# Unequal gaps between the eight split weight buffers of a two-block transformer kernel

## The chip, the cores and the metric

The kernel runs on one core of a Trainium2 chip. The metric is the device time of one launch in microseconds (us); the time before is the median of three runs. Traces are of one profiled execution of the same program.

## The reference

Two transformer blocks over 256 tokens of 2048 features, all in float32. Cut to the products that matter here:

```python
h = modulate(rmsnorm(x, g_norm_mix[l]), shift_m, scale_m)
proj = h @ w_in[l]                        # q, k, v of two kinds of attention
...
x = x + gate_m[:, None, :] * (jnp.concatenate([o_diff, o_mla], axis=-1) @ w_out[l])
h = modulate(rmsnorm(x, g_norm_ffn[l]), shift_f, scale_f)
f = jnp.square(jax.nn.relu(h @ w_ff1[l])) @ w_ff2[l]
...
xn = _rms(x, norm_attn[l])                # second block
... = jnp.split(xn @ w_in[l], points, axis=-1)
merged = jax.nn.sigmoid(gate_a) * (o_a @ w_up_fox[l]) + jax.nn.sigmoid(gate_b) * (o_b @ w_up_nsa[l])
x = x + merged @ w_out[l]
hn = _rms(x, norm_ffn[l])
x = x + (jax.nn.silu(hn @ w_ffn_gate[l]) * (hn @ w_ffn_up[l])) @ w_ffn_down[l]
```

All weight matrices together are some 550 MB, and each is used once for all 256 tokens.

## The kernel before

Weights stream through in tiles of 128 partitions by up to 1024 float32 numbers, 512 KB each, in the order of one list (`plan`). `load` issues the transfer of a tile from SyncE into a raw buffer. `split_next` makes two parts of it in the type float32r: ScalarE copies the raw tile into `wh` (line 117, the high part), and VectorE subtracts (line 118: `wl = raw - wh`, the low part). `get` hands a split tile to `linear`, and splits the tiles behind it ahead of their use.

`linear` holds two accumulators in PSUM, one for each 128 tokens (`tt`). For each split tile, for both `tt` and for both halves `kk` of the tile (each holds 128 rows of the weight, 512 columns wide or fewer), `mm3` issues three matmuls (lines 132, 133, 134): high activation by high weight, high activation by low weight, low activation by high weight. So one tile makes 12 matmuls in a row, in four rounds of three. The activation, 128 columns, is the stationary operand (`lhsT`); the weight is the moving one (`rhs`), of 512 columns or fewer. Every matmul has a weight load (LDWEIGHTS) of its own, which TensorE does while the matmul ahead of it streams. In the trace a matmul reads `acc<-wh,Ah`: output, moving operand, stationary operand.

The activations are held split too, as pairs: `Ah`, `Al` (the normalized input of a projection), `midh`, `midl` and `mid2h`, `mid2l` (the hidden layers of the two feed-forward parts), `O2h`, `O2l` (attention output of the second block), `Mh`, `Ml` (the merged heads). One product has the roles reversed: in `q_nope` the activation `cqh`, `cql` moves, 256 columns, and the weight is stationary. Attention itself uses plain float32 operands.

Buffers lie in SBUF one behind another in the order in which their pools are opened. The split weight buffers are four `wh` and four `wl` of 4096 bytes a partition, in the pool `whl`; behind it come the pools of `x`, of `Ah` and `Al`, of small tiles, and those of each stage. A pool with several buffers of one tag deals them out in turn. The start of each in bytes, as the built program has it:

| tiles | first start | modulo 512 | modulo 64 |
|---|---|---|---|
| `wh` (4), `wl` (4), each 4096 behind the one ahead | 46368, 62752 | 288 | 32 |
| `Ah`, `Al` | 95520, 111904 | 288 | 32 |
| `cqh`, `midh`, `midl`, `mid2h`, `mid2l`, `O2h`, `O2l`, `Mh`, `Ml` | 191424, 180160, 196544, 141248, 157632, 133056, 149440, 165824, 182208 | 448 | 0 |

Slices within a tile begin at multiples of 64 bytes behind its start; those of the 512-column weight tiles and of the 128-column stationary operands at multiples of 512.

Of the kernel before, what the change touches and what calls it, by code (L numbers as in the profile page):

```python
# [9 lines left out]
F32 = mybir.dt.float32  # L10
# [6 lines left out]
P = 128  # L17
# [15 lines left out]
class HL:  # L33
    """A float32 operand held as the exact sum of two float32r parts."""
# [8 lines left out]
class Kernel:  # L43
    def __init__(self, ctx, tc, a, out, offs):
        self.tc, self.nc, self.a, self.out, self.offs = tc, tc.nc, a, out, offs
        self.ctx = ctx
        pool = lambda name, bufs, **k: ctx.enter_context(tc.tile_pool(name=name, bufs=bufs, **k))
        self.const = pool("const", 1)
        self.wraw = pool("wraw", RAW_BUFS)
        self.whl = pool("whl", SPLIT_BUFS)  # L50
        self.xp = pool("xp", 1)
        self.ap_ = pool("ap", 1)
        self.sm = pool("sm", 4)
        self.ps_acc = pool("ps_acc", 4, space=bass.MemoryType.PSUM)
        self.ps_tr = pool("ps_tr", 2, space=bass.MemoryType.PSUM)
        self.ps_at = pool("ps_at", 2, space=bass.MemoryType.PSUM)
        ctx.enter_context(tc.manual_schedule())
        self.fillers = []
        self.done = set()
        self.now = 0  # L60
        self.budget = 2
        self.ahead = 2

    # ---------------------------------------------------------------- helpers
# [16 lines left out]
    def rsqrt(self, ms, n, tag, pool=False):  # L81
        """ms ** -0.5: a first guess from the exponent, then three Newton steps."""
        v = self.nc.vector
        e = self.nc.gpsimd if pool else v
        ti = self.tiny("rs_i", n, I32)
        v.tensor_scalar(ti, ms.bitcast(I32), 1, None, op0=OP.logical_shift_right)
        y = self.tiny(tag, n)
        v.tensor_scalar(y.bitcast(I32), ti, -1.0, 1597463007.0, op0=OP.mult, op1=OP.add)
        h = self.tiny("rs_h", n)
        v.tensor_scalar(h, ms, -0.5, None, op0=OP.mult)  # L90
        t = self.tiny("rs_t", n)
        cols = [slice(i, i + 1) for i in range(n)]
        for _ in range(3):
            if n <= 2:
                for c in cols:
                    e.tensor_scalar(t[:, c], y[:, c], y[:, c], h[:, c], op0=OP.mult, op1=OP.mult)  # L96
                for c in cols:
                    e.tensor_scalar(y[:, c], t[:, c], 1.5, y[:, c], op0=OP.add, op1=OP.mult)  # L98
            else:
                e.tensor_mul(t, y, y)  # L100
                e.tensor_mul(t, t, h)
                if pool:
                    e.tensor_scalar(t, t, 1.5, None, op0=OP.add)
                    e.tensor_mul(y, y, t)
                else:
                    v.scalar_tensor_tensor(y, t, 1.5, y, op0=OP.add, op1=OP.mult)
        return y
# [6 lines left out]
    def split(self, dst, src, scale=None):  # L114
        """dst (HL) = src * scale, rounded to its two parts."""
        if scale is None:
            self.nc.scalar.activation(dst.hi, src, AF.Copy)  # L117
            self.nc.vector.tensor_sub(dst.lo, src, dst.hi.bitcast(F32))  # L118
        else:
            self.nc.scalar.activation(dst.hi, src, AF.Copy, scale=scale)  # L120
            self.nc.vector.scalar_tensor_tensor(dst.lo, src, scale, dst.hi.bitcast(F32),
                                                op0=OP.mult, op1=OP.subtract)
# [6 lines left out]
    def mm3(self, out, x, w, start, stop):  # L129
        """out += x.T @ w from the parts of x and w."""  # L130
# [9 lines left out]
    # ---------------------------------------------------------- weight stream  # L140
    def start_stream(self, plan):
        self.plan = plan
        self.dma_ptr = 0
        self.split_ptr = 0
        self.use_ptr = 0
        self.raw = {}
        self.ready = {}
        self.load()
# [14 lines left out]
    def split_next(self):  # L163
# [6 lines left out]
        else:  # L170
            hi = self.whl.tile([P, 1024], F32R, tag="wh", name="wh")
            lo = self.whl.tile([P, 1024], F32R, tag="wl", name="wl")
# [15 lines left out]
    def get(self):  # L188
        """The next weight tile; the ones behind it are split ahead of their use."""
# [6 lines left out]
    # ------------------------------------------------------ the conditioning  # L196
    def ada_part(self, e, src):
        """One tile of w_ada: feature by partition on VectorE, or k by partition on TensorE."""
# [36 lines left out]
    def row_of(self, sec, pool):  # L235
        """A gate, held feature by partition, as the same row in every partition."""
# [14 lines left out]
    # -------------------------------------------------------------- schedule  # L251
# [42 lines left out]
    # ------------------------------------------------------------- linear job  # L294
    def linear(self, groups, w, evac, acc=None, first=True, last=True, needs={}):
        """acc[tt] += sum over the groups' k tiles; groups: lists of HL [128, 256]."""
# [20 lines left out]
    # ------------------------------------------------------------------ setup  # L317
# [67 lines left out]
    def rope(self, x, cos, sin, slots, tmp):  # L385
        """x [128, slots, 2h] in place; cos, sin [128, 2h]; tmp [128, 2, slots, 2h]."""
# [10 lines left out]
    # ---------------------------------------------------- norm and modulation  # L397
# [4 lines left out]
    # ================================================================ block 1  # L402
    def x_hat(self, kg, r, xh):
        """512 features of the normalized x."""
# [4 lines left out]
    def x_hat_T(self, b, xh):  # L409
        """Two feature tiles of xh, transposed in one bank."""  # L410
# [6 lines left out]
    def modulate(self, A, kt, n, src, which, h):  # L417
        """A[:, kt .. kt + n - 1] = the two parts of src * scale + shift."""
# [25 lines left out]
    def block1_attention_proj(self):  # L444
# [12 lines left out]
        with ExitStack() as e2:  # L457
# [112 lines left out]
            # q_nope of all heads, transposed  # L570
# [12 lines left out]
            # q_rope  # L583
# [45 lines left out]
    def p_transpose_evac(self, blocks, dst, n):  # L629
        """blocks: (column offset, in_) transposed into one bank; dst [*, n] copied from it."""  # L630
# [42 lines left out]
    def diff_head(self, h, pj, O, wp, kab):  # L673
# [54 lines left out]
        for tt in range(2):  # L728
            junk = wp.tile([P, P], F32, tag="jk", name="jk", bufs=2)
# [12 lines left out]
    def block1(self):  # L742
# [26 lines left out]
        # output projection, in the order in which the heads end  # L769
# [46 lines left out]
    def ffn1(self, r):  # L816
# [46 lines left out]
        def ff1_start():  # L863
            """The first three column blocks, a quarter of their rows at a time."""
# [63 lines left out]
    def r12_gen(self, ss):  # L928
        """The two norms of x, the second from the first: r1 and r1 * r2."""
# [23 lines left out]
    def xT_gen(self, A, j, gain, key):  # L953
        """A[:, 4j .. 4j+3] from the 512 columns of x, times the gain."""
# [12 lines left out]
    # ================================================================ block 2  # L967
# [21 lines left out]
    def rms_heads(self, pj, n, heads, key, width):  # L989
        """pj [128, 2, >= n * width] in place: each of n heads of width normalized."""  # L990
# [14 lines left out]
    def key_gen(self, pj, kcat, br, gain, key):  # L1005
        """ks or kw: normalize, transpose into kcat[:, g, kb, (kt, br, 128)]."""
# [15 lines left out]
    def flat_gen(self, src, F, nt, kind, key):  # L1022
        """F (HL [128, nt, 48]) = the blocks of the compression, feature-major."""
# [475 lines left out]
    # -------------------------------------------------------------- the order  # L1499
    def make_plan(self):  # L1500
# [19 lines left out]
        def even(main, side):  # L1520
            """side spread evenly over main."""
# [71 lines left out]
def insert2(s, step):  # L1593
    """Every step-th column of s [128, n]."""
# [9 lines left out]
def layout(inp):  # L1604
    """The inputs as the program reads them: values moved, none changed."""
# [15 lines left out]
    A = {}  # L1621
# [111 lines left out]
```

## Time and profile before

| | before |
|---|---|
| time, median of 3 runs (lowest, highest) | 2742.49 us (2740.55, 2745.44) |
| span of the profiled execution, first to last instruction | 2742.6 us |
| TensorE matmul busy | 2675.7 us, 98% |
| TensorE weight load busy | 2219.3 us, 81% |
| VectorE, ScalarE, GpSimd busy | 1699.0, 1244.4, 82.9 us |
| mean granted TensorE clock | 0.991 of 2.4 GHz |

The span of the profiled execution equals the median to 0.1 us, so a sum made against the one holds for the other. A matmul's busy time in the trace reaches from its start to its modelled end, and matmuls overlap: how long one takes in a row of many is read from the distance of two starts, not from its busy time.

### The profile page before, as it was taken

Reading aid. Unit: us, or ns where it says so; the run is one execution under the profiler, and the core shown is the slowest. Engines: PE = TensorE matmul, PEld = TensorE weight load, DVE = VectorE, ACT = ScalarE, POOL = GpSimd, SP = SyncE. Lnnn points to the kernel's source line nnn. Section 1 sums busy time; section 2 is a strip of 40 time slices with the busy share of each in tenths; the row PEclk is TensorE's granted clock in tenths of the full one; section 3 lists DMA queues with packets and bytes.
Section 4 is the critical chain, followed back from the end, with each engine's and each line's share of the span. In section 5 each row is a group of like instructions: output and inputs, shape, how many; then the busy total and the mean of one; then the engine's idle time right before and its main releaser. Section 6 shows DMA issues by size and latency. Waiting matters only on the chain.

```text
span 2742.6 us, 34412 instructions
## 1 busy us (share of the span) xinstructions
PE 2675.7 (98%) x12646; PEld 2219.3 (81%) x12646; DVE 1699.0 (62%) x2761; ACT 1244.4 (45%) x1791; POOL 82.9 (3%) x151
## 2 busy tenths in 40 slices
PE   7999999899999999999999999999999999999999
PEld 3588977688888888878898998888888888888887
DVE  5587877866666555667766665555554545454555
ACT  3255654344444444454655554444444343434443
POOL 0002320000000000002000000000000000000000
PEclk9999999999999999999999999999999999999999
DMA  9977777667777655545733555656556665666564
GB/s 351 331 268 272 262 256 276 243 225 234 232 236 231 215 191 185 183 163 161 251 124 99 162 180 181 189 190 189 180 188 188 187 192 188 190 189 192 185 191 146
DMA packets 163608, 568.85 MB, mean 207 GB/s; under 512 B 18288, under 2 KB 18544, under 8 KB 162800
## 3 DMA queue, kind: packets, MB, share of 16 engines
q1 hardware_dynamic: 160992, 558.70, 61.6%
q10 hardware_dynamic: 2448, 7.97, 0.7%
q8 instruction: 99, 1.62, 0.2%
q14 instruction: 69, 0.57, 0.1%
HBM read 564.50 MB, written 2.10 MB: 207 GB/s over the span
## 4 chain that ended last, share of the span: by engine, by line
PE 83%; DVE 6%; issue 4%; ACT 3%; POOL 2%; DMA 2%; SPq 0%; ACTq 0%; DVEq 0%; POOLq 0%
PE acc L133 25%; PE acc L132 25%; PE acc L134 25%; PE tr L138 2%; DVE wl L118 2%; POOL rs_t L96 2%; PE tr L206 2%; ACT wh L117 1%; DVE ajunk L222 1%; DMA raw<-ada_scale_m 1%; PE at L1160 1%; POOL r_d L98 0%; DMA raw<-ff 0%; DMA x<-x 0%; PE at L132 0%
## 5 line engine op out<-in xcount | busy, mean ns | idle before, releaser
L118 DVE TENSOR_TENSOR wl<-raw,wh 128x1024 fp32r<-128x1024 f32 (+3 forms) x926 | 1071.5, 1164 | 831.7 <-ACT wh L117 826.1
L117 ACT ACTIVATE wh<-raw 128x1024 fp32r<-128x1024 f32 (+3 forms) x926 | 930.7, 1011 | 982.8 <-PE acc L134 917.7
L132 PE MATMUL acc<-wh,Ah 128*128 128x512 f32 (+2 forms) x2400 | 912.8, 380 | 6.7 <-ACT Ah L117 5.1
L133 PE MATMUL acc<-wl,Ah 128*128 128x512 f32 (+2 forms) x2400 | 896.0, 373 | 8.3 <-DVE wl L118 8.2
L134 PE MATMUL acc<-wh,Al 128*128 128x512 f32 (+2 forms) x2400 | 895.2, 373 | 0.5 <-DVE Al L118 0.5
L132 PEld LDWEIGHTS acc<-wh,Ah 128*128 128x128 f32 x2400 | 453.7, 189 | 84.7 <-issue 10.2
L133 PEld LDWEIGHTS acc<-wl,Ah 128*128 128x128 f32 x2400 | 453.8, 189 | 76.3 <-DVE wl L118 12.1
L134 PEld LDWEIGHTS acc<-wh,Al 128*128 128x128 f32 x2400 | 453.2, 189 | 66.4 <-DVE Al L118 2.0
L133 PE MATMUL acc<-wl,midh 128*128 128x512 f32 x512 | 204.2, 399 | 0.8 <-DVE wl L118 0.8
L132 PE MATMUL acc<-wh,midh 128*128 128x512 f32 x512 | 202.8, 396 | 0.3 <-ACT midh L117 0.2
L222 DVE SCALAR_TENSOR_TENSOR ajunk<-raw,silu_row 128x1024 bf16<-128x1024 f32 x160 | 195.1, 1219 | 12.2 <-ACT silu_row L249 10.6
L134 PE MATMUL acc<-wh,midl 128*128 128x512 f32 x512 | 201.2, 393 | 0.0
L133 PE MATMUL acc<-wl,mid2h 128*128 128x512 f32 x352 | 140.5, 399 | 0.0
L132 PE MATMUL acc<-wh,mid2h 128*128 128x512 f32 x352 | 139.2, 395 | 0.0
L134 PE MATMUL acc<-wh,mid2l 128*128 128x512 f32 x352 | 138.0, 392 | 0.0
L132 PEld LDWEIGHTS acc<-wh,midh 128*128 128x128 f32 x512 | 96.1, 188 | 25.0 <-ACT midh L117 0.5
L133 PEld LDWEIGHTS acc<-wl,midh 128*128 128x128 f32 x512 | 96.2, 188 | 23.4 <-DVE wl L118 1.6
L134 PEld LDWEIGHTS acc<-wh,midl 128*128 128x128 f32 x512 | 96.1, 188 | 23.3 <-DVE midl L118 0.4
L132 PEld LDWEIGHTS acc<-wh,mid2h 128*128 128x128 f32 x352 | 66.1, 188 | 17.0
L134 PEld LDWEIGHTS acc<-wh,mid2l 128*128 128x128 f32 x352 | 66.1, 188 | 15.8
L133 PEld LDWEIGHTS acc<-wl,mid2h 128*128 128x128 f32 x352 | 66.1, 188 | 15.0
L133 PE MATMUL acc<-wl,O2h 128*128 128x512 f32 (+1 forms) x208 | 73.3, 352 | 0.3 <-DVE wl L118 0.3
(430 smaller groups left out, 2159.8 us busy)
## 6 DMA issues: line engine op xcount, KB each, us to landing
raw<-ff SPq DMA_DIRECT2D x256, 512.0 KB, 4.3
raw<-f2g SPq DMA_DIRECT2D x88, 512.0 KB, 3.6
raw<-f2u SPq DMA_DIRECT2D x88, 512.0 KB, 3.6
raw<-f2d SPq DMA_DIRECT2D x88, 512.0 KB, 3.8
raw<-wo SPq DMA_DIRECT2D x64, 512.0 KB, 4.3
raw<-wi_d SPq DMA_DIRECT2D x64, 384.0 KB, 4.4
raw<-w_fox SPq DMA_DIRECT2D x64, 384.0 KB, 3.3
raw<-ada_scale_m SPq DMA_DIRECT2D x32, 512.0 KB, 6.8
```

The costliest lines, as they stand in the source:

```text
L96: e.tensor_scalar(t[:, c], y[:, c], y[:, c], h[:, c], op0=OP.mult, op1=OP.mult)
L117: self.nc.scalar.activation(dst.hi, src, AF.Copy)
L118: self.nc.vector.tensor_sub(dst.lo, src, dst.hi.bitcast(F32))
L132: mm(out, lhsT=x.hi, rhs=w.hi, start=start, stop=False)
L133: mm(out, lhsT=x.hi, rhs=w.lo, start=False, stop=False)
L134: mm(out, lhsT=x.lo, rhs=w.hi, start=False, stop=stop)
L138: self.nc.tensor.transpose(out, in_, self.ident[0:n, 0:n])
L206: self.nc.tensor.matmul(self.ada_row[0:1, :], lhsT=self.silu_c[:, kt:kt + 1], rhs=src[:, kk * 512:(kk + 1) * 512], start=kt == 0, stop=kt ...
L222: v.scalar_tensor_tensor(junk, src, 1.0, self.silu_row[:, (k % 2) * 1024:(k % 2 + 1) * 1024], op0=OP.mult, op1=OP.mult, accum_out=self.ada ...
L1160: mm(ps1, lhsT=qT[:, kb, P:T], rhs=kcat[:, g, kb].rearrange("p t b k -> p (t b k)"), start=kb == 0, stop=kb == 1)
```

## The change

The pool `whl` no longer deals out four buffers of each tag. It holds eight tiles of their own names (`wha`, `wla`, `whb`, ... `wld`), taken in turn by a counter, and ahead of six of them lies an empty tile of 32 to 192 bytes. The gaps make 544 bytes together; all pools behind `whl` begin 544 bytes later. To make room for them, a scratch tile of 512 bytes (`jk`, line 729, the squares of an attention output on ScalarE, of which only the sum is used) has one buffer in place of two. Comments and docstrings went as well, which moves line numbers: lines 132 to 134 are 133 to 135 in the changed kernel, 117 and 118 are 118 and 119.

```diff
-        self.whl = pool("whl", SPLIT_BUFS)
+        self.whl = pool("whl", 1)
+        self.split_ptr_w = 0
...
+        for b, hi_pad, lo_pad in (("a", 0, 32), ("b", 32, 64), ("c", 0, 96), ("d", 128, 192)):
+            for part, pad in (("wh" + b, hi_pad), ("wl" + b, lo_pad)):
+                if pad:
+                    self.whl.tile([P, pad // 4], F32, tag="gap_" + part, name="gap_" + part)
+                self.whl.tile([P, 1024], F32R, tag=part, name=part)
         self.load()
...
-            hi = self.whl.tile([P, 1024], F32R, tag="wh", name="wh")
-            lo = self.whl.tile([P, 1024], F32R, tag="wl", name="wl")
+            b = "abcd"[self.split_ptr_w % SPLIT_BUFS]
+            self.split_ptr_w += 1
+            hi = self.whl.tile([P, 1024], F32R, tag="wh" + b, name="wh" + b)
+            lo = self.whl.tile([P, 1024], F32R, tag="wl" + b, name="wl" + b)
...
-            junk = wp.tile([P, P], F32, tag="jk", name="jk", bufs=2)
+            junk = wp.tile([P, P], F32, tag="jk", name="jk", bufs=1)
```

Where the tiles start in the changed program:

| tile | start | modulo 512 | modulo 64 |
|---|---|---|---|
| `wha`, `wla` | 46368, 50496 | 288, 320 | 32, 0 |
| `whb`, `wlb` | 54624, 58784 | 352, 416 | 32, 32 |
| `whc`, `wlc` | 62880, 67072 | 416, 0 | 32, 0 |
| `whd`, `wld` | 71296, 75584 | 128, 320 | 0, 0 |
| `Ah`, `Al` | 96064, 112448 | 320 | 0 |
| `cqh`, `midh`, `mid2h`, `O2h`, `Mh` and their low parts | 544 later than before | 480 | 32 |

No engine's instructions change their order, and their number stays. On TensorE, in the second block's feed-forward part, seven matmuls at the turn from one weight tile to the next read before:

```order
9011 L132 MATMUL acc_18207<-wh_18150,mid2h_17240 128x512
9012 L133 MATMUL acc_18207<-wl_18151,mid2h_17240 128x512
9013 L134 MATMUL acc_18207<-wh_18150,mid2l_17241 128x512
9014 L132 MATMUL acc_18206<-wh_18168,mid2h_17240 128x512
9015 L133 MATMUL acc_18206<-wl_18169,mid2h_17240 128x512
9016 L134 MATMUL acc_18206<-wh_18168,mid2l_17241 128x512
9017 L132 MATMUL acc_18206<-wh_18168,mid2h_17240 128x512
```

The same place in the changed program:

```order
9011 L133 MATMUL acc_18221<-whc_18164,mid2h_17254 128x512
9012 L134 MATMUL acc_18221<-wlc_18165,mid2h_17254 128x512
9013 L135 MATMUL acc_18221<-whc_18164,mid2l_17255 128x512
9014 L133 MATMUL acc_18220<-whd_18182,mid2h_17254 128x512
9015 L134 MATMUL acc_18220<-wld_18183,mid2h_17254 128x512
9016 L135 MATMUL acc_18220<-whd_18182,mid2l_17255 128x512
9017 L133 MATMUL acc_18220<-whd_18182,mid2h_17254 128x512
```

Nothing has moved; the moving operand now comes from a named buffer of a set of eight, each with a start of its own.

## Rows read from the trace of the kernel before

**Rows 1.** The page's first, second and fourth parts: busy time of each engine, the granted TensorE clock in 40 slices of the span, and the chain that ended last.
```profile
PE 2675.7 (98%) x12646; PEld 2219.3 (81%) x12646; DVE 1699.0 (62%) x2761; ACT 1244.4 (45%) x1791; POOL 82.9 (3%) x151
PEclk9999999999999999999999999999999999999999
PE 83%; DVE 6%; issue 4%; ACT 3%; POOL 2%; DMA 2%; SPq 0%; ACTq 0%; DVEq 0%; POOLq 0%
PE acc L133 25%; PE acc L132 25%; PE acc L134 25%; PE tr L138 2%; DVE wl L118 2%; POOL rs_t L96 2%; PE tr L206 2%; ACT wh L117 1%; DVE ajunk L222 1%; DMA raw<-ada_scale_m 1%; PE at L1160 1%; POOL r_d L98 0%; DMA raw<-ff 0%; DMA x<-x 0%; PE at L132 0%
```

**Rows 2.** Busy time of each engine in eight stretches of the span; columns: the stretch, its length, busy us and instructions of each engine, granted clock, share of the DMA engines, GB/s.
```profile
0.00:50.00 50.00, 32.55 (x102) 13.35 (x103) 29.21 (x86) 19.27 (x36) 0.50 (x5) 0.95 0.97 381
50.00:100.00 50.00, 47.95 (x185) 24.22 (x184) 27.41 (x50) 10.65 (x15) 0.00 (x0) 0.99 0.86 316
100.00:200.00 100.00, 93.06 (x483) 73.66 (x482) 74.18 (x152) 42.05 (x66) 0.00 (x0) 0.95 0.81 293
200.00:300.00 100.00, 93.23 (x504) 83.77 (x503) 82.70 (x183) 60.00 (x153) 23.59 (x30) 0.97 0.72 250
300.00:600.00 300.00, 279.92 (x1325) 232.66 (x1324) 236.04 (x402) 149.85 (x271) 38.26 (x67) 0.97 0.73 258
600.00:1000.00 400.00, 400.00 (x1770) 326.62 (x1770) 251.62 (x281) 167.25 (x174) 0.00 (x0) 1.00 0.69 226
...
1500.00:2000.00 500.00, 499.94 (x2422) 431.26 (x2422) 287.79 (x528) 233.51 (x321) 0.00 (x0) 1.00 0.56 179
2000.00:2500.00 500.00, 500.00 (x2222) 411.35 (x2221) 257.59 (x245) 211.84 (x219) 4.66 (x13) 1.00 0.61 189
```

**Rows 3.** Groups of TensorE's matmuls by line and shape; columns: line, engine, operation, out<-moving,stationary, rows*columns of the stationary operand, output shape, count, busy us and mean ns of one, idle time before them and its releaser.
```profile
L132 PE MATMUL acc<-wh,Ah 128*128 128x512 f32 x1632 | 642.1, 393 | 5.1 <-ACT Ah L117 5.1
L132 PE MATMUL acc<-wh,Ah 128*128 128x384 f32 x704 | 250.6, 356 | 1.6 <-ACT wh L117 1.6
L132 PE MATMUL acc<-wh,midh 128*128 128x512 f32 x512 | 202.8, 396 | 0.3 <-ACT midh L117 0.2
L132 PE MATMUL acc<-wh,mid2h 128*128 128x512 f32 x352 | 139.2, 395 | 0.0
L132 PE MATMUL acc<-wh,Mh 128*128 128x512 f32 x128 | 50.7, 396 | 0.0
L132 PE MATMUL acc<-wh,O2h 128*128 128x512 f32 x128 | 50.6, 395 | 0.0
L1160 PE MATMUL at<-kcat,nqT 96*128 96x512 f32 x32 | 15.0, 592 | 0.0
```

**Rows 4.** TensorE in order of time where the stationary operand is `A`, 512 columns; columns: start in us, busy us, line, operation.
```profile
2184.19 0.39 PE L132 MATMUL acc<-wh,Ah 128*128 128x512 f32 x1
2184.42 0.39 PE L133 MATMUL acc<-wl,Ah 128*128 128x512 f32 x1
2184.64 0.39 PE L134 MATMUL acc<-wh,Al 128*128 128x512 f32 x1
2184.87 0.39 PE L132 MATMUL acc<-wh,Ah 128*128 128x512 f32 x1
```

**Rows 5.** The same where the stationary operand is `mid2` (rounds of three, 34 us earlier).
```profile
2150.40 0.39 PE L134 MATMUL acc<-wh,mid2l 128*128 128x512 f32 x1
2150.63 0.39 PE L132 MATMUL acc<-wh,mid2h 128*128 128x512 f32 x1
2150.86 0.40 PE L133 MATMUL acc<-wl,mid2h 128*128 128x512 f32 x1
2151.10 0.39 PE L134 MATMUL acc<-wh,mid2l 128*128 128x512 f32 x1
```

**Rows 6.** The same where the activation `cq` moves, 256 columns, and the weight is stationary: eight matmuls and the one behind them.
```profile
183.02 0.28 PE L132 MATMUL acc<-cqh,wh 128*128 128x256 f32 x1
...
183.97 0.28 PE L134 MATMUL acc<-cqh,wl 128*128 128x256 f32 x1
```

**Rows 7.** The same at the turn from `mid2` to `A`: the first matmul by `A`, the tenth, and the first of four plain float32 matmuls in a row elsewhere (512 columns, four together in one row).
```profile
2181.43 0.40 PE L132 MATMUL acc<-wh,Ah 128*128 128x512 f32 x1
...
2183.51 0.39 PE L132 MATMUL acc<-wh,Ah 128*128 128x512 f32 x1
...
1397.35 1.88 PE L1160 MATMUL at<-kcat,nqT 96*128 96x512 f32 x4
```

**Rows 8.** Weight loads at `mid2` and at `A`, the matmul that streams during the second of them, and two matmuls of 384 columns by `A`, three apart: start, busy us.
```profile
2178.40 0.19 PEld L132 LDWEIGHTS acc<-wh,mid2h 128*128 128x128 f32 x1
2183.74 0.19 PEld L134 LDWEIGHTS acc<-wh,Al 128*128 128x128 f32 x1
2183.74 0.39 PE L133 MATMUL acc<-wl,Ah 128*128 128x512 f32 x1
1380.36 0.33 PE L132 MATMUL acc<-wh,Ah 128*128 128x384 f32 x1
1380.88 0.33 PE L132 MATMUL acc<-wh,Ah 128*128 128x384 f32 x1
```

**Rows 9.** What VectorE waits for most, TensorE's two longest entries of waits for the split, and the scratch tile `jk` on ScalarE (min/median/max ns).
```profile
DVE wl L118 <- ACT wh L117: 826.1, 650, 5.8
PE acc L133 <- DVE wl L118: 9.2, 11, 2.4
L730 ACT ACTIVATE jk<-on x16: 303/309/337, 240.9 to 407.2; 128x128 f32<-128x128 f32 x16
```

## The prediction

> **What bounds the kernel now.** I read the page's shares first. TensorE's matmuls cover 98% of the span and the chain that ended last lies on TensorE for 83% of it, three quarters of the span on the three lines of `mm3` [rows 1]. The clock is granted in full, 2.4 GHz, from 600 us on, and nearly so before [rows 2]. Then the stretches: from 600 us on TensorE leaves hardly a gap, while VectorE is busy for some 55 to 65% and the DMA engines for 56 to 69%; only the first 100 us, with 32.6 and 48.0 of 50 us busy at a DMA share of 0.97 and 0.86, wait for weights, and the stretch from 300 to 600 us has 20 us of gaps [rows 2]. The split is no bound: VectorE waits 826 us for ScalarE, but TensorE waits only 9 us in all for the low part [rows 9]. So time is set by how close one matmul follows another on TensorE.
>
> That distance is where this change can act, so I read it from starts. With `A` stationary, three matmuls of 512 columns take 2184.87 - 2184.19 = 0.68 us, 226.7 ns each [rows 4]. With `mid2` stationary, the same three lines take 2151.10 - 2150.40 = 0.70 us, 233.3 ns each [rows 5]. At 2.4 GHz 512 columns stream in 213.3 ns, so the two have 13.3 and 20.0 ns over. With 384 columns and `A`, 0.52 us for three are 173.3 ns, against 160 ns of columns: 13.3 ns over again [rows 8]. The excess doesn't grow with the columns that stream; it is a cost for each matmul and its weight load. The weight load itself takes 0.19 us in both cases and begins with the matmul ahead of it, so it ends in time [rows 8], yet something of it costs the stream. Shape, type, line and weight buffer of the two cases are alike; what differs is where the stationary operand starts: 32 past a multiple of 64 bytes for `A`, as the weights, and a multiple of 64 for `mid2`. I take that as the cause; the trace doesn't prove it.
>
> Two more rows give the scale. Where `cq` moves from a multiple of 64 and the weight, 32 past one, is stationary, eight matmuls of 256 columns take 0.95 us, 118.8 ns each, against 106.7 ns: 12.1 ns over [rows 6]. And plain float32 matmuls, which take two steps for a column, have almost nothing over: four of 512 columns take 1.88 us to the end of the last, whose own time is 592 ns [rows 3], so (1880 - 592) / 3 = 429 ns each against 426.7, 2.7 ns over [rows 7].
>
> **The change part by part.** *Instructions.* None is added, removed or moved, so no queue is passed and no transfer is issued earlier. The eight named buffers are dealt out in the same turn of four as before, so the split still waits for the matmuls that read the buffer four tiles earlier; cost nothing. *The scratch tile.* The 16 squares of 309 ns that write `jk` [rows 9] stand on ScalarE in their order anyway, so one buffer adds no wait on another engine. Were each pair to serialize by a full instruction, 8 x 0.3 = 2.4 us of ScalarE, 45% busy [rows 1], would be hidden under TensorE. *The elementwise work.* ScalarE and VectorE write the same sizes to other addresses. The trace has no row for them at another residue; 826 us of VectorE's waits stand between a change of a few per cent there and TensorE [rows 9]. I take nothing.
>
> *The matmuls.* Of the twelve that a tile makes, two in three read the high part and one the low. Counting the starts modulo 64: buffer a gives two at 32 and one at 0 in each round, b three at 32, c two at 32 and one at 0, d three at 0. So 7 of 12 matmuls stream from 32 past a multiple and 5 of 12 from a multiple. The stationary operands swap: `A` goes from 32 to 0, and `mid`, `mid2`, `O2`, `M` go from 0 to 32. That gives four relations, three of which the trace shows: both at 32 costs 13.3 ns (`A` now), weight at 32 and activation at 0 costs 20.0 (`mid2` now), moving at 0 and stationary at 32 costs 12.1 (`cq` now). The fourth, both at 0, is not there. From below it is bounded by the 2.7 ns of the float32 matmuls, from above by the 20.0 of `mid2`. I take 13.3 - (20.0 - 12.1) = 5.4 ns, an estimate that adds what moving to 0 saves between the second and the third case to the first.
>
> Then for `A`: 7/12 x 20.0 + 5/12 x 5.4 = 13.9 ns, 0.6 more than now. Its matmuls are (1632 + 704) x 3 = 7008 [rows 3], of which some 200 in the first stretches wait for weights in any case, so 6800 x 0.6 = +4 us. For the others: 7/12 x 13.3 + 5/12 x 12.1 = 12.8 ns, 7.2 less; there are (512 + 352 + 128 + 128) x 3 = 3360 [rows 3], so -24 us. The few hundred matmuls of 256 to 320 columns are left out. The sum is -20 us, and 2742.6 - 20 = 2722 us.
>
> The bounds: with every matmul at 2.7 ns over, 6800 x 10.6 + 3360 x 17.3 = 130 us are saved, 2612 us. With every matmul at 20.0, `A` loses 6800 x 6.7 = 46 us and the rest stays, 2788 us. What hides nothing here is the weight stream: at 20 us less its transfers run 0.7% denser, and the DMA share of 0.56 to 0.69 [rows 2] has room for that.
>
> A rule speaks against the whole sum. The 233.3 and 226.7 ns of rows 4 and 5 say that a weight load costs the running stream 13 to 20 ns. The Trainium skill says the opposite, in "TensorE: Matmul & The Clock Gate" (Part 2, step 1) and "SBUF — State Buffer" (Who interferes with whom): TensorE reads the moving operand and the weights through two independent ports, so that loading the next weights takes nothing from the running matmul, and it waits for no other reader. By that rule the starts of the buffers would be worth nothing, and the sum 0; the trace disagrees on the excess, since the first page's gap of N/2.4 + 2.5 ns (Back-to-back issue gap) would be 215.8 ns.
>
> **The rivals.** *The rhythm is lost (slower).* Behind a turn from `mid2` to `A` the first nine matmuls by `A` take 2183.51 - 2181.43 = 2.08 us, 231.1 ns each, before they settle at 226.7 [rows 7]: 4.4 ns each until weight load and stream have found a cheap rhythm. Now all weight buffers have one residue, so the rhythm outlasts the turn of a buffer. With eight unlike starts each round of three and each tile could begin it anew. At 4.4 ns on all 10160 matmuls that is +45 us on top of the sum, 2767 us. It decides the sign from 20/45 on: if more than about 5 of the 12 matmuls of a tile run unsettled. For it speaks that nine is near twelve; against it, that `mid2` has no cheap rhythm now to lose. *The residue is not the cause.* The excess may come from elsewhere, distance in the memory for one, or gains and losses may cancel: 2742 us. For it, that two cases at 0 and 32 are few; against it, that `mid`, `mid2`, `M` and `O2`, at four places, have nearly one busy time, 395 to 396 ns, and `A` has 393 [rows 3]. *Spread starts are cheap as such.* If it is the equal start that makes load and stream meet, spreading may bring all matmuls to the middle of 5.4 and 13.3, 9.4 ns: 6800 x 3.9 + 3360 x 10.6 = 62 us, 2680 us. Only the estimate of 5.4 speaks for it.
>
> **How the numbers follow.** The forecast has 0.42, lost rhythm 0.25, cheap spread 0.18, no effect 0.15. The likeliest gives 2722 us, with 2705 to 2738 as its own range, since 5.4 may be 2.7 or 12. The range that leaves out 2 in 10 reaches from a little below the cheap spread to the lost rhythm: 2673 to 2767 us; the bounds of 2612 and 2788 lie outside. Within 0.2%, 5.5 us, a measurement of this kernel can't tell a change from none. Faster: nine tenths of the forecast and all of the cheap spread, with a little of the rest, 0.58. Same: most of the no-effect case and an edge of the forecast, 0.14. Slower: 0.28.
>
> **What would show it.** In the trace after, rounds of three by `mid2` should take 0.68 us on average, down from 0.70, and those by `A` 0.68 to 0.69, unevenly: long on buffers a to c and about 0.656 on buffer d, where both operands start at a multiple of 64. If `A` has 0.69 or more on all buffers, the rhythm was lost; if both keep 0.68 and 0.70, the residue isn't the cause. The forecast fails if the fourth relation is as dear as the second, or if the gaps between starts depend on residues larger than 64.

## The result and the profile after

The changed kernel takes 2761.24 us (median of 4 runs, 2759.92 to 2763.82); the kernel before took 2743.3 us (median of 4) beside it. The ratio is 1.0068 with a 95% interval of 1.0054 to 1.0083: slower by 0.7%, some 18 us, where 0.7% less was forecast. The profiled execution of the changed kernel took 2760.53 us, its span 2758.8 us.

The page of the changed kernel, its first, second and fourth parts, which answer to [rows 1]:

```profile
PE 2692.0 (98%) x12646; PEld 2219.5 (80%) x12646; DVE 1699.6 (62%) x2761; ACT 1244.5 (45%) x1791; POOL 82.8 (3%) x151
PEclk9999999999999999999999999999999999999999
PE 52%; DVE 1%; issue 0%; ACT 0%; DVEq 0%; ACTq 0%
PE acc L133 16%; PE acc L134 16%; PE acc L135 16%; PE tr L139 1%; PE at L1168 0%; PE at L1165 0%; PE tr L1172 0%; DVE wld L119 0%; DVE jk L1005 0%; PE at L1245 0%; PE at L1265 0%; PE at L1229 0%; ACT whd L118 0%; PE at L1217 0%; DVE wlc L11
```

Counts are the same on every engine. VectorE, ScalarE and GpSimd are busy for the same time to 0.6 us, the clock is granted nearly in full, and TensorE's matmuls are busy for 16 us more. Nothing else moved; what the change costs, it costs on TensorE. (The shares of the chain add up to 53%: it was followed back over about half of the span, so they are lower throughout than in [rows 1].)

The stretches of the changed kernel, columns as in [rows 2]:

```profile
600.00:1000.00 400.00, 400.00 (x1755) 324.68 (x1755) 250.70 (x279) 166.15 (x174) 0.00 (x0) 1.00 0.68 224
...
2000.00:2500.00 500.00, 500.00 (x2189) 405.68 (x2189) 253.52 (x241) 208.65 (x216) 4.66 (x13) 1.00 0.60 187
```

TensorE is busy throughout at the full clock, as before, but it gets through fewer matmuls: 1755 where there were 1770, and 2189 where there were 2222 [rows 2].

The pace itself, from starts on TensorE: the first and last of 155 matmuls by `mid2` in an unbroken row, of 228 by `A` behind them (with the first of the tile on buffer d and of the tile behind it), and of 107 by `A` with 384 columns (start, busy us):

```profile
2290.23 0.39 PE L134 MATMUL acc<-wlb,mid2h 128*128 128x512 f32 x1
...
2325.97 0.39 PE L135 MATMUL acc<-whb,mid2l 128*128 128x512 f32 x1
2326.20 0.40 PE L133 MATMUL acc<-whc,Ah 128*128 128x512 f32 x1
...
2328.97 0.39 PE L133 MATMUL acc<-whd,Ah 128*128 128x512 f32 x1
...
2331.76 0.39 PE L133 MATMUL acc<-wha,Ah 128*128 128x512 f32 x1
...
2378.91 0.40 PE L135 MATMUL acc<-wha,Al 128*128 128x512 f32 x1
...
1287.02 0.34 PE L134 MATMUL acc<-wld,Ah 128*128 128x384 f32 x1
...
1305.54 0.34 PE L135 MATMUL acc<-whd,Al 128*128 128x384 f32 x1
```

`mid2`: 35.74 us over 154 distances, 232.1 ns, where there were 233.3 [rows 5]. `A`: 52.71 / 227 = 232.2 ns, where there were 226.7 [rows 4]. `A` with 384 columns: 18.52 / 106 = 174.7 ns, where there were 173.3 [rows 8]. The changed kernel has lost the short distance of `A` with 512 columns and won little with the others.

On buffer d the prediction expected some 219 ns for `A`; the tile shown takes 2.79 us for twelve, 232.5 ns. Over all tiles in unbroken rows `A` has 232.2, 232.4, 231.7 and 232.8 ns on buffers a to d, and `mid2` 232.1, 231.2, 231.3 and 233.4.

### The profile page after: what moved, and what is told of

Same layout as the page of the kernel before. It is cut to its first block, busy times and chain, and to the rows that moved or that the text cites. A ratio compares the mean times of both kernels' runs of the same rounds, so it can differ in the third digit from the quotient of the medians.

```text
span 2758.8 us, 34409 instructions
## 1 busy us (share of the span) xinstructions
PE 2692.0 (98%) x12646; PEld 2219.5 (80%) x12646; DVE 1699.6 (62%) x2761; ACT 1244.5 (45%) x1791; POOL 82.8 (3%) x151
## 4 chain that ended last, share of the span: by engine, by line
PE 52%; DVE 1%; issue 0%; ACT 0%; DVEq 0%; ACTq 0%
PE acc L133 16%; PE acc L134 16%; PE acc L135 16%; PE tr L139 1%; PE at L1168 0%; PE at L1165 0%; PE tr L1172 0%; DVE wld L119 0%; DVE jk L1005 0%; PE at L1245 0%; PE at L1265 0%; PE at L1229 0%; ACT whd L118 0%; PE at L1217 0%; DVE wlc L119 0%
## 5 line engine op out<-in xcount | busy, mean ns | idle before, releaser
L119 DVE TENSOR_TENSOR wld<-raw,whd 128x1024 fp32r<-128x1024 f32 (+3 forms) x231 | 268.9, 1164 | 261.7 <-ACT whd L118 261.0
L119 DVE TENSOR_TENSOR wla<-raw,wha 128x1024 fp32r<-128x1024 f32 (+1 forms) x232 | 270.1, 1164 | 225.9 <-ACT wha L118 221.8
L119 DVE TENSOR_TENSOR wlc<-raw,whc 128x1024 fp32r<-128x1024 f32 (+3 forms) x231 | 268.8, 1164 | 182.5 <-ACT whc L118 182.4
L119 DVE TENSOR_TENSOR wlb<-raw,whb 128x1024 fp32r<-128x1024 f32 (+1 forms) x232 | 270.0, 1164 | 173.5 <-ACT whb L118 173.4
L118 ACT ACTIVATE whd<-raw 128x1024 fp32r<-128x1024 f32 (+3 forms) x231 | 233.4, 1010 | 297.6 <-PE acc L135 280.4
L118 ACT ACTIVATE whc<-raw 128x1024 fp32r<-128x1024 f32 (+3 forms) x231 | 233.2, 1010 | 262.5 <-PE acc L135 239.9
L118 ACT ACTIVATE wha<-raw 128x1024 fp32r<-128x1024 f32 (+1 forms) x232 | 234.1, 1009 | 232.5 <-PE acc L135 223.3
L118 ACT ACTIVATE whb<-raw 128x1024 fp32r<-128x1024 f32 (+1 forms) x232 | 234.0, 1009 | 206.0 <-PE acc L135 190.0
L133 PE MATMUL acc<-whb,Ah 128*128 128x512 f32 (+1 forms) x600 | 231.6, 386 | 1.7 <-ACT whb L118 1.6
L133 PE MATMUL acc<-whc,Ah 128*128 128x512 f32 (+2 forms) x600 | 231.3, 385 | 1.8 <-ACT Ah L118 1.8
L133 PE MATMUL acc<-wha,Ah 128*128 128x512 f32 (+1 forms) x600 | 229.0, 382 | 2.8 <-ACT Ah L118 2.8
L135 PE MATMUL acc<-whc,Al 128*128 128x512 f32 (+2 forms) x600 | 226.7, 378 | 0.4 <-DVE Al L119 0.4
```

The costliest lines, as they stand in the source:

```text
L133: mm(out, lhsT=x.hi, rhs=w.hi, start=start, stop=False)
L135: mm(out, lhsT=x.lo, rhs=w.hi, start=False, stop=stop)
```

## The experiments

Every experiment leaves the computation as it is and moves addresses by empty tiles. "Difference" below is the start of the activation minus the start of the weight buffers. Where the pool of the weights is left as it was, its eight buffers all have the same start modulo 512.

### The two halves of the change, and equal starts

`k1_shift_only` has the weights as before and moves everything behind them by 544 bytes, as the change does:

```diff
-        self.xp = pool("xp", 1)
+        self.gapp = pool("gap", 1); self.gapp.tile([P, 136], F32, tag="gap", name="gap"); self.xp = pool("xp", 1)
...
-            junk = wp.tile([P, P], F32, tag="jk", name="jk", bufs=2)
+            junk = wp.tile([P, P], F32, tag="jk", name="jk", bufs=1)
```

> The kernel before with its eight weight buffers at equal starts (288 modulo 512) and all tiles behind them 544 bytes later, as in the change: A starts at 320, mid, mid2, O2, M at 480 modulo 512. Theory R (unequal weight starts break a settled rhythm): starts of the weights are equal, so each class settles; the steady distance of two matmuls by A and by mid lies on one value each, within 226.7 to 233.3 ns, and nothing wanders with the weight buffer; the ratio to before is below 1.004. Theory S (the activation's own start modulo 64 counts): A 233.3 ns, mid and mid2 226.7 ns, 6800 x 6.6 - 3360 x 6.6 = +23 us, ratio 1.008.

Measured: 2756.25 us, ratio 1.0052 (1.0037 to 1.0067), between the two theories. Its `mid2` and `A`, first and last of an unbroken row of 155 and of 228:

```profile
2286.95 0.39 PE L133 MATMUL acc<-wl,mid2h 128*128 128x512 f32 x1
...
2322.21 0.40 PE L134 MATMUL acc<-wh,mid2l 128*128 128x512 f32 x1
2322.44 0.40 PE L132 MATMUL acc<-wh,Ah 128*128 128x512 f32 x1
...
2375.41 0.39 PE L134 MATMUL acc<-wh,Al 128*128 128x512 f32 x1
```

`A` takes 52.97 / 227 = 233.3 ns, `mid2` 35.26 / 154 = 229.0 ns. With all weights alike, so with nothing unlike inside a round or between tiles, `A` has lost its short distance too: a steady difference of 32 bytes is enough. `mid2`, at a difference of 192, has a price that is neither of the two known ones.

`k2_gaps_only` is the change with its last gap cut from 192 to 160 bytes, so that the gaps make 512 bytes and all activations keep their starts modulo 512:

```diff
-        for b, hi_pad, lo_pad in (("a", 0, 32), ("b", 32, 64), ("c", 0, 96), ("d", 128, 192)):
+        for b, hi_pad, lo_pad in (("a", 0, 32), ("b", 32, 64), ("c", 0, 96), ("d", 128, 160)):
```

> The changed kernel with the last gap 160 in place of 192 bytes, so that the gaps make 512 and A and all stage tiles keep the starts modulo 512 of the kernel before (288 and 448); seven of the eight weight buffers start as in the change, wld 32 bytes earlier. Theory R: A 231 to 233 ns as in the change, mid and mid2 231 to 234, ratio 1.006 to 1.011. Theory S by the prediction's table: A 226 ns, mid 7/12 x 20 + 5/12 x 5.4 over 213.3 = 227 ns, ratio 0.991.

Measured: 2763.35 us, ratio 1.0080 (1.0065 to 1.0095). `A` keeps the start that it had before and yet takes 52.69 / 227 = 232.1 ns:

```profile
2329.51 0.40 PE L133 MATMUL acc<-whc,Ah 128*128 128x512 f32 x1
...
2382.20 0.40 PE L135 MATMUL acc<-wha,Al 128*128 128x512 f32 x1
```

So the activation's own start isn't what counts. The halves don't add up: some 14 us the shift, 21 us the gaps, 18 us both.

`k3_same` takes the kernel before and brings `mid`, `mid2`, `O2` and `M` to the start of the weights:

```diff
+        fp = es.enter_context(self.tc.tile_pool(name="ffn1", bufs=1)); fp.tile([P, 88], F32, tag="gap", name="gap")
...
+        bp = es.enter_context(self.tc.tile_pool(name="b2", bufs=1)); bp.tile([P, 88], F32, tag="gap", name="gap")
...
+        fp = es.enter_context(self.tc.tile_pool(name="ffn2", bufs=1)); fp.tile([P, 88], F32, tag="gap", name="gap")
```

> The kernel before with 352 bytes ahead of the tiles of the two feed-forward stages and of the second block, so that mid, mid2, O2 and M start at 288 modulo 512, as A and the weights do. Theories R and S: all of them settle at A's 226.7 ns, 3360 x 6.6 = 22 us less, ratio 0.992. If the start is not the cause of the 233.3 ns: 233.3 stays, ratio 1.000.

Measured: 2719.01 us, ratio 0.9919 (0.9903 to 0.9936): faster than both kernels, by three empty tiles of 352 bytes.

```profile
2259.69 0.40 PE L133 MATMUL acc<-wl,mid2h 128*128 128x512 f32 x1
...
2294.61 0.39 PE L134 MATMUL acc<-wh,mid2l 128*128 128x512 f32 x1
2294.84 0.39 PE L132 MATMUL acc<-wh,Ah 128*128 128x512 f32 x1
...
2346.29 0.39 PE L134 MATMUL acc<-wh,Al 128*128 128x512 f32 x1
...
2000.00:2500.00 500.00, 500.00 (x2240) 414.85 (x2239) 256.85 (x237) 212.99 (x217) 0.00 (x0) 1.00 0.63 192
```

`mid2` takes 34.92 / 154 = 226.8 ns and `A` 51.45 / 227 = 226.7: one price for all. The last row is the stretch from 2000 to 2500 us: 2240 matmuls where there were 2222 before [rows 2] and 2189 after, at the same clock.

### The price by difference

Three kernels set the starts of the other activations one by one, with plain weight buffers. Their edit is that of `k3_same` with other sizes, and a fourth empty tile at the start of the pool `merge`. In bytes (`ffn1` moves `mid`, `b2` moves `O2` and `M`, `merge` moves `M` further, `ffn2` moves `mid2`):

| kernel | `ffn1` | `b2` | `merge` | `ffn2` | elsewhere |
|---|---|---|---|---|---|
| `k4_scan` | 384 | 416 | 64 | 448 | |
| `k5_scan2` | 64 | 96 | 32 | 160 | |
| `k6_scan3` | 224 | 256 | 32 | 320 | 32 in front of the weights, 480 behind them, one `jk` |

> The kernel before with the activations of each stage at a distance of their own from the weights modulo 512: mid 32, O2 64, M 128, mid2 96 (A stays at 0). Theory S (modulo 64): O2 and M 226.7 ns, mid and mid2 233.3 ns. Theory R says only that each stage settles on one repeating round of three, at its own value; a value under 226.7 ns would show a start that is better than the kernel's.

> Empty tiles set the starts of the other activations 224 (mid), 256 (O2), 288 (M) and 320 (mid2) bytes behind those of the weights, modulo 512; A stays equal to the weights. So far the settled distance of 512-column matmuls by that difference is 226.8 ns at 0, 233.3 at 32, 233.2 at 64, 234.2 at 96, 232.7 at 128, 233.4 at 160, 229.0 at 192. Theory E (equal starts are the only cheap ones): these four classes take 229 to 235 ns, A stays at 227, and the run takes 2730 to 2745 us. Theory H (the price runs in a curve that falls from 160 on, with its lowest point half of 512 away): mid and O2 take less than 226 ns, and the run takes under 2715 us.

> The weights start 32 bytes later (320) and A stays at 288, a difference of 480; mid lies 352, O2 384, M 416 and mid2 448 bytes behind the weights, modulo 512. Theory E: every class takes 229 to 235 ns; with A at 2 to 8 ns above its 226.8 on some 6800 matmuls the run takes 2745 to 2790 us. Theory N (it is the sign that counts: an activation that starts a little ahead of the weights is as cheap as an equal one): A stays at or under 227 ns, and the run takes under 2740 us.

Measured, one execution each: 2742.76, 2739.59 and 2769.86 us. Two of the rows from which the prices come, `O2` (48 matmuls) in the second and `A` (228) in the third:

```profile
1728.76 0.39 PE L132 MATMUL acc<-wh,O2h 128*128 128x512 f32 x1
...
1739.41 0.39 PE L134 MATMUL acc<-wh,O2l 128*128 128x512 f32 x1
```

```profile
2336.34 0.40 PE L132 MATMUL acc<-wh,Ah 128*128 128x512 f32 x1
...
2389.31 0.39 PE L134 MATMUL acc<-wh,Al 128*128 128x512 f32 x1
```

`O2`, at a difference of 256, takes 10.65 / 47 = 226.6 ns, as cheap as equal; `A`, at 480, takes 233.3, which is what `mid` takes at 224. Worked out in the same way from unbroken rows of up to 252 matmuls in all runs:

| difference, bytes | ns for one matmul of 512 columns | where |
|---|---|---|
| 0 | 226.7 | `A` before; all five in `k3_same` |
| 32 | 233.3 | `A` in `k1`, `mid` in `k4` |
| 64 | 233.4 | `O2` in `k4` |
| 96 | 234.2 | `mid2` in `k4` |
| 128 | 232.3 | `M` in `k4` |
| 160 | 233.4 | `mid`, `mid2`, `O2`, `M` before |
| 192 | 229.0 | the same four in `k1` |
| 224 | 233.3 | `mid` in `k5` |
| 256 | 226.7 | `O2` in `k5` |
| 288, 320 | 233.3, 233.3 | `M`, `mid2` in `k5` |
| 352, 384, 416 | 234.3, 232.2, 233.4 | `mid`, `O2`, `M` in `k6` |
| 448, 480 | 228.9, 233.3 | `mid2`, `A` in `k6` |

The second half repeats the first to 0.1 ns: the price goes by the difference modulo 256. At 128, though, rows with the same addresses differ: two of `M`'s five in `k4` have 233.3 in place of 232.3, and one of `O2`'s eight in `k6` has 233.2 in place of 232.2. The places themselves don't count: 32 is 320 against 288 in `k1` and `k4` and, a period on, 64 against 288 in `k5`; 224 is 0 against 288 in `k5` and, a period on, 288 against 320 in `k6`; each has one price. Equal is the cheapest of the eight. The theory of a smooth curve with its low point half of 512 away holds for one point only: 256 is cheap because it is equal again.

`k11_fine` looks between: the same activations inside wider tiles, so that they start 4 to 28 bytes behind the weights, modulo 256.

```diff
+        o = {"mid": 1, "mid2": 2, "O2": 4, "M": 7}.get(tag, 0)
+        if o and shape[1] * shape[2] >= 1024:
+            a, b = shape[1:]
+            hi, lo = (pool.tile([P, a * b + 64], F32R, tag=tag + p, name=tag + p, bufs=bufs)[:, o:o + a * b].rearrange("p (a b) -> p a b", a=a) for p in "hl")
+            return HL(hi, lo)
```

> Plain buffers; the activations start 4 (mid), 8 (mid2), 16 (O2) and 28 bytes (M) behind the weights, modulo 256; A equal. Theory E (equal is the lowest point): all four at 226.7 to 233.5 ns, 2717 to 2743 us. Theory G (the load begins 3 to 4 cycles after the stream, so the lowest point lies a few bytes off equal): at least one of them under 226 ns. Theory B (the memory is met in pieces of 32 bytes): all four at 226.7, or all but M.

Measured: 2735.87 us, one execution. `mid2`, 8 bytes behind:

```profile
2272.78 0.39 PE L138 MATMUL acc<-wl,mid2h 128*128 128x512 f32 x1
...
2308.31 0.39 PE L139 MATMUL acc<-wh,mid2l 128*128 128x512 f32 x1
```

That is 35.53 / 154 = 230.7 ns; in the same way 4 bytes give 232.4. Nothing is below equal, so the theory of a low point a few bytes off falls, and that of pieces of 32 bytes too. (The weight load, which the first of them puts 3 to 4 cycles behind the stream, begins 2 to 4 ns behind it in the traces before and of `k3_same`.)

At 16 and 28 bytes the difference alone doesn't fix the price. `O2`, 16 behind, in its first row, whose second matmul is the first shown, and in its second:

```profile
1661.75 0.40 PE L138 MATMUL acc<-wl,O2h 128*128 128x512 f32 x1
...
1672.48 0.40 PE L139 MATMUL acc<-wh,O2l 128*128 128x512 f32 x1
...
1694.49 0.39 PE L137 MATMUL acc<-wh,O2h 128*128 128x512 f32 x1
...
1705.15 0.39 PE L139 MATMUL acc<-wh,O2l 128*128 128x512 f32 x1
```

The first, behind the attention, takes 10.73 / 46 = 233.3 ns; the second, directly behind a row by `A`, 10.66 / 47 = 226.8, and so do the other six. At a difference of 256, in `k5_scan2`, the first row has 226.7 too. `M`, 28 behind, takes 226.7 for 36 matmuls directly behind `O2`, and 233.3 to 234.9 in its other four rows, each behind transposes. With the same addresses the pace thus differs by what came ahead. That it is taken over from there would fit; no run tests it.

### What unlike buffers do among themselves

`k10_gaps256` has the named buffers of the change, with gaps that leave all starts equal modulo 256, and the activations of `k3_same`:

```diff
+        for part, pad in (("wha", 0), ("wla", 0), ("whb", 256), ("wlb", 0), ("whc", 0), ("wlc", 0), ("whd", 256), ("wld", 0)):
```

> The eight named weight buffers of the change, with gaps of 256 bytes in front of whb and whd alone, and empty tiles that bring the activations to the same start as the weights modulo 256. So far the settled distance by the difference of starts repeats after 256 bytes (O2 at 256: 226.7 ns, as at 0; mid2 at 448: 228.9, as 229.0 at 192). Theory P (only the difference modulo 256 between streamed and loaded operand counts): all classes of 512 columns at 226.7 to 227 ns, 2716 to 2722 us, as with the plain buffers at equal starts (2719 us). Theory U (spread or named buffers cost something by themselves): above 2730 us.

Measured: 2720.67 us, ratio 0.9918 (0.9902 to 0.9935), all five classes at 226.7 to 226.8 ns. Names, gaps and the single `jk` cost nothing by themselves: `k3_same`, without them, has 2719.01.

`k7_tiles` makes tiles unlike one another, and nothing inside a tile:

```diff
+        for part, pad in (("wha", 0), ("wla", 0), ("whb", 0), ("wlb", 0), ("whc", 96), ("wlc", 0), ("whd", 0), ("wld", 0)):
...
+            b = "acbd"[self.split_ptr_w % SPLIT_BUFS]
```

> Named buffers dealt in the order a, c, b, d: a and b start equal to all activations modulo 256, c and d 96 bytes further, so that every turn of a weight tile changes the difference between 0 and 160, and inside a tile it is constant. Theory P (each pair pays by its own difference): 226.7 and 233.4 ns in turn, 230.0 on average, 3.3 more than all equal on some 8200 matmuls of 512 columns, about 2719 + 27 = 2746 us. Theory R (a turn breaks the rhythm and it takes four to nine matmuls to settle): above 231.5 ns on average, the equal tiles at 229 or more, over 2758 us.

Measured: 2765.0 us, one execution, and 232.1 ns for `A` over the row of 228: above the second theory's limits of 2758 us and 231.5 ns. A tile at a difference of 160 (`whd`), an equal one (`wha`) and the turn to the next, by starts:

```profile
2479.96 0.40 PE L132 MATMUL acc<-whd,Ah 128*128 128x512 f32 x1
...
2482.78 0.40 PE L132 MATMUL acc<-wha,Ah 128*128 128x512 f32 x1
...
2484.63 0.39 PE L134 MATMUL acc<-wha,Al 128*128 128x512 f32 x1
2484.86 0.39 PE L132 MATMUL acc<-wha,Ah 128*128 128x512 f32 x1
2485.08 0.39 PE L133 MATMUL acc<-wla,Ah 128*128 128x512 f32 x1
2485.31 0.39 PE L134 MATMUL acc<-wha,Al 128*128 128x512 f32 x1
2485.54 0.40 PE L132 MATMUL acc<-whc,Ah 128*128 128x512 f32 x1
```

The unlike tile takes 2.82 / 12 = 235.0 ns for each matmul (234.5 over all tiles on c and d). The equal one takes 1.85 / 8 = 231.3 for its first eight, and only its last four come near the cheap distance (0.91 / 4 by rows of two decimals; over all tiles in `wha` these four places have 226.7 to 227.7, and the whole tile 229.9). Then the next tile ends it. It looks like the settling of [rows 7], eight or nine matmuls long, in each tile anew.

`k9_parts` makes the low weights unlike the high ones, and the activations in three ways:

```diff
+            if "gapw" not in self.done:
+                self.done.add("gapw")
+                self.whl.tile([P, 24], F32, tag="gap", name="gap", bufs=1)
             lo = self.whl.tile([P, 1024], F32R, tag="wl", name="wl")
...
+        gap = {"mid": 96, "M": 96, "mid2": 160}.get(tag)
+        if gap and tag not in self.done:
+            self.done.add(tag)
+            pool.tile([P, gap // 4], F32, tag="gap2", name="gap2", bufs=1)
```

> The low weights start 96 bytes behind the high ones (modulo 256). A and O2: both parts equal to the high weights. mid and M: high part equal to the high weights, low part to the low ones. mid2: the other way round. Theory L (what counts is the stream against the weight load that runs beside it, which is that of the next matmul): A and O2 two pairs in three at 0 and one at 160, 229.0 ns; mid and M all pairs at 0, 226.7; mid2 two at 96 and one at 160, 233.9; about 2738 us. Theory O (a matmul's own two operands count): A and O2 229.0 as well; mid and M one each at 0, 160 and 96, 231.4; mid2 one at 96 and two at 0, 229.2. Theory R (any unlikeness inside a round of three breaks the rhythm): all five classes at 231 to 234.

Measured: 2753.01 us, one execution. One round by `mid`, and the ends of 228 matmuls by `A`, of 36 by `mid2` directly behind a row by `A`, and of 155 by `mid2` behind transposes:

```profile
668.34 0.39 PE L138 MATMUL acc<-wh,midl 128*128 128x512 f32 x1
668.56 0.39 PE L136 MATMUL acc<-wh,midh 128*128 128x512 f32 x1
...
669.02 0.39 PE L138 MATMUL acc<-wh,midl 128*128 128x512 f32 x1
```

```profile
2454.46 0.40 PE L136 MATMUL acc<-wh,Ah 128*128 128x512 f32 x1
...
2506.92 0.39 PE L138 MATMUL acc<-wh,Al 128*128 128x512 f32 x1
...
2273.51 0.40 PE L136 MATMUL acc<-wh,mid2h 128*128 128x512 f32 x1
...
2281.75 0.39 PE L138 MATMUL acc<-wh,mid2l 128*128 128x512 f32 x1
...
2283.09 0.40 PE L137 MATMUL acc<-wl,mid2h 128*128 128x512 f32 x1
...
2318.94 0.39 PE L138 MATMUL acc<-wh,mid2l 128*128 128x512 f32 x1
```

`mid` has one short distance in three (0.22 us; 224.3 ns over all its rounds) and two of 231.3, 228.9 on average over a row of 155; `A` has 52.46 / 227 = 231.1, `mid2` 35.85 / 154 = 232.8 in the long rows and 235.7 over the five rows of 36, 233.3 on average. The order of the three is that of the theory of stream and next load (226.7, 229.0, 233.9). `mid2` speaks against that of a matmul's own two operands (229.2), and `mid`, with `M` at 229.1, against that of a broken rhythm (231 to 234 for all). But the sizes aren't met: where unlike distances alternate, a matmul doesn't take the price that its own difference has in a steady row. That stays open.

### Both operands at a multiple of 64

`k12_all_at_0` is the fourth relation of the prediction, alone and steady: 32 bytes in front of the weights, and empty tiles that make all activations, `cq` too, equal to them modulo 256.

```diff
+        self.gap0 = pool("gap0", 1); self.gap0.tile([P, 8], F32, tag="gap", name="gap"); self.whl = pool("whl", SPLIT_BUFS)
...
+            tp = e2.enter_context(self.tc.tile_pool(name="lat", bufs=1)); tp.tile([P, 24], F32, tag="gap", name="gap")
```

The other three empty tiles are those of `k3_same`.

> Plain buffers, one empty tile of 32 bytes in front of the weights and empty tiles that bring all activations, cq too, to the same start as the weights modulo 256; all of them start at a multiple of 64. This is the fourth relation of the prediction, both operands at 0, steady and alone. Theory D (only the difference of the starts counts, equal is cheap): 226.7 ns for every class of 512 columns, about 2719 us as with all at 32 past a multiple. Theory of the prediction (starts at a multiple of 64 are cheap in themselves, 5.4 ns over the columns): 218.7 ns, about 2655 us.

Measured: 2720.13 us, ratio 0.9919 (0.9902 to 0.9935). The ends of 228 matmuls by `A`, and of nine in a row in which `cq` moves:

```profile
2297.33 0.39 PE L132 MATMUL acc<-wh,Ah 128*128 128x512 f32 x1
...
2348.79 0.39 PE L134 MATMUL acc<-wh,Al 128*128 128x512 f32 x1
...
183.06 0.28 PE L132 MATMUL acc<-cqh,wh 128*128 128x256 f32 x1
...
184.02 0.28 PE L134 MATMUL acc<-cqh,wl 128*128 128x256 f32 x1
```

`A` takes 51.46 / 227 = 226.7 ns: 13.4 over its columns, not 5.4. And `cq`, now equal to the weights, takes 0.96 us for eight where it took 0.95 [rows 6]. With 256 columns and the weight as the stationary operand equal starts save nothing.

## Why the prediction was wrong

**What bounds the kernel was read rightly.** Time is set by how close one matmul follows another; the changed kernel differs from the one before in little else, and a kernel that changes nothing else gains 23 us by it. The added names, the single `jk`, the split and the weight stream cost nothing that shows, as the sum had them (`k10_gaps256`). (One share was misread: VectorE is busy for 52% of the stretch from 2000 to 2500 us [rows 2], not for 55 to 65; the argument doesn't need it.)

**The step that failed is the cause that was read out of two cases.** The two stationary operands, 32 past a multiple of 64 for `A` and at a multiple for `mid2`, differ in something else as well: `A` and the weights start at 288 modulo 512, all three alike, and `mid2` at 448. The prediction put the price on each start by itself, modulo 64. The scan shows that in steady rows it lies on the difference of the two, modulo 256. That `mid`, `mid2`, `M` and `O2` have one price at four places, which was counted for the residue, is as true of the difference: all four have 160.

**The estimate for both at a multiple of 64** (5.4 ns) added what the case of `cq` seemed to save. Measured, steady, it is 13.4 ns where the two are equal (`k12_all_at_0`), and more where both are at a multiple of 64 but not equal: in `k6_scan3` `O2` has 232.2 - 213.3 = 18.9 and `mid2` 15.6. The case of `cq` doesn't carry over: a moving operand at 0 with a stationary one at 32 costs 20.0 for `A` in `k6_scan3`, not 12.1. The upper bound that the prediction kept for it, 20.0, was nearly right; had it been used in the sum, `A` would have cost 46 us and the sum +22.

**The terms.** For `A` the sum had +4 us; measured, 232.2 - 226.8 = 5.4 ns on some 4900 distances of 512 columns are 26 us, and 1.4 ns on some 2100 of 384 columns 3 us. For the others it had -24 us; measured, 232.0 - 233.4 = -1.4 ns on some 3360 are -5 us. Together +24, of which some 18 us show. Counted over the whole of both traces, from each matmul's start to the next matmul's, pauses included, `A` with 512 columns takes 4.7 ns more and not 5.4, 23 us; the others take 5 us less; and `A` with 384 columns takes 0.2 ns less: there the pauses between rows gave back what the rows took longer.

**The rival "the rhythm is lost" named the right loser.** `A` had a cheap rhythm and lost it on all buffers, the sign of this in the prediction's own list, and its 2767 us lie 6 us above the result. Its reason, unlike starts that begin the rhythm anew in each tile, is real: in `k7_tiles` it alone turns an expected 230.0 into 232.1. But operands that are no longer equal are enough to lose it: `k1_shift_only` has 233.3 for `A` without any mixing. How the two share the result here isn't shown. By the table of steady prices, with each stream taken against the load that runs beside it, the changed buffers would give `A` 231.1, 233.3, 233.4 and 228.2 ns on a to d, 231.5 on average against 232.2 measured, and the others 232.6 against 232.0. The averages are near, the buffers are not: `A` is dearest on d (232.8), where the table has it cheapest. That some 4.8 of the 5.4 ns come from unequal operands and some 0.7 from the mixing is thus an estimate for the average alone, by prices that don't hold buffer by buffer. For 384 columns it is the other way about: a steady difference costs nothing there (18.38 us for 106 distances in `k1_shift_only`, 173.4 ns as before), and in that row the kernels with unlike buffers are slower, 174.7 after and 175.9 in `k7_tiles`.

**The rival "spread starts are cheap"** falls: of all steady differences that were tried, none is below equal, and no kernel with unlike buffers is faster than its like with equal ones. **"The residue is not the cause"** was right in its letter and wrong in what it concluded, no effect.

The rule that the prediction set against its sum, that the load and the stream of TensorE don't disturb each other, would have given no change. The runs from 2719 to 2770 us, whose kernels differ in addresses and in nothing else that was seen to cost time, show that it matters where the two lie to each other. That it is the load beside the stream that counts, and not the matmul's own, rests on the order in `k9_parts` alone. Why the difference counts modulo 256, and what the 13.3 ns over the columns are that remain when all starts are equal, stays open.

## What to carry to other kernels

Where a matmul and the weight load beside it follow each other without a gap, read the distance of starts for each pair of tiles and put the start addresses next to it, all of them, before a cause is chosen from two cases: two tiles that differ in one residue differ in others too. Here float32r operands of 512 moving columns want the moving and the stationary tile to start at the same place modulo 256 bytes, and three empty tiles that see to it are worth 0.8%. A pattern that settles over eight or nine matmuls is mostly lost if something changes every twelve.

## What was not expected of the hardware

- The time of a matmul in a full row depends on where its operands lie in the memory: 226.7 to 234.3 ns for the same 512 columns, by the difference of the starts modulo 256 bytes, the same to 0.1 ns when the difference grows by 256 (at 128 for most rows).
- The dependence isn't smooth: 226.7 ns at 0, 232.4 at 4 bytes, 230.7 at 8, 233.3 at 32, 229.0 at 192.
- The same addresses can hold two paces: at 16 bytes 226.7 ns in seven rows and 233.4 in one, at 28 bytes 226.7 in one row and 233.3 to 234.9 in four (`k11_fine`).
- Single distances go below the best steady one: 224.3 ns for one matmul in three of `mid` in `k9_parts`, paid back by 231.3 for the other two. Whether a mixture exists that is cheaper than 226.7 on average was not tried further.
- With 384 columns a steady difference of 32 bytes costs nothing in a long row, and with `cq` moving 256 columns equal starts gain nothing.
